# First GEMM stage in plain float32, and the conditioning row read from HBM: one change to a two-layer encoder kernel

## The chip, the cores and the metric

The kernel runs on one core of a Trainium2 chip. The metric is device time in microseconds (us) of one execution; a kernel's time is the median of its runs.

## The reference, cut to what matters

```python
cond = jax.nn.silu(c)                                   # c: (1, 2048)
for l in range(2):
    mod = (cond @ ada_w[l] + ada_b[l])[:, None, :]      # 2048 -> 6 * 2048
    sh1, sc1, g1, sh2, sc2, g2 = jnp.split(mod, 6, axis=-1)
    h = rmsnorm(x, norm_mix_g[l]) * (1 + sc1) + sh1     # x: (1, 256, 2048)
    m = hybrid_mixer(h, ...) if l == 0 else mamba2_bidirectional(h, ...)
    x = x + g1 * m
    h = rmsnorm(x, norm_ffn_g[l]) * (1 + sc2) + sh2
    x = x + g2 * squared_relu_mlp(h, ffn_w1[l], ffn_w2[l])
return rmsnorm(x, final_norm_g)
```

All inputs are float32. `hybrid_mixer` begins with `h @ w_in`; the first GEMM stage of the kernel works out the 2048 of its columns that make `v` (1024) and the two latents (512 each).

## The kernel before

Activations lie feature-major: `x` is 16 tiles of 128 features by 256 tokens. Weights come from HBM in chunks of 1024 KB ([128, 2048] float32, `load`, line 164), one DMA each on SyncE's queue, in one fixed order, into a ring of slots (`slot`, line 153): three in a permanent pool and some that a stage adds. A slot is loaded again when its last reader is done, and the queue issues in order.

Products are made with split operands. `next_half` (line 169) cuts a chunk into halves: ScalarE rounds a half to the matmul's fast float32 form (`whi`, line 177), and VectorE subtracts to get the rest (`wlo`, line 179). The activation is split the same way into the two planes of an `A` tile (`split_into`, line 281). A product is then three fast matmuls: high by high, high by low, low by high. `look` lets halves be made some way ahead of their products.

The modulation `cond @ ada_w` is done mostly on VectorE: for each of 192 tiles of the transposed `ada_w` (1024 KB each), `ada_sum` (line 323) multiplies by the row `cond`, which stands on all 128 partitions, and sums along the row in one instruction (line 325). `spread_cond` (line 126) makes that row twice, at the start and in layer 1 (line 1120): for each of 16 groups of 128 features, VectorE scales the identity by a column of silu(c) (line 132), TensorE multiplies it by a constant matrix (line 133), and ScalarE copies four results at a time from PSUM (line 134).

The stage that the change is about is `start` (line 533). Its contraction has 16 steps `kt`, a step being one chunk of `w_st`: columns 0 to 1023 for v, 1024 to 2047 for the latents. In each step `feed` keeps the normed tiles two ahead: for tile t, `by_tile` (line 450) has the two modulation tiles (scale, then shift) loaded and summed, adds the biases in three tiny VectorE instructions, and `h_tile` (line 413) makes the normed, scaled, shifted tile (VectorE line 415, ScalarE line 422) and its split (lines 282, 283). Then TensorE does v with the activation stationary and 512 weight columns moving (12 matmuls, line 569), and the latents with the weights stationary and 256 tokens moving (24 matmuls, line 204). So a step takes three loads of 1024 KB. In steps 14 and 15 the first three tiles of the next modulation rows are queued too. The raw ring has 8 slots here (3 permanent, 3 from the layer's pool, 2 from the stage's pool `sp`).

The order of instructions on each engine is set by a scheduler that lists them by its own estimates, within the program's dependences; each engine then runs its list in order.

Of the kernel before, what the change touches and what calls it, by code (L numbers as in the profile page):

```python
# [25 lines left out]
# columns of the packed per-feature parameters  # L26
# [11 lines left out]
# columns of the packed constants  # L38
# [4 lines left out]
# the modulation row that the tensor engine works out  # L43
ON_PE = (0, G1)
# the rows whose bias comes with the tile's use
# [4 lines left out]
def tile_trunk(  # L50
# [3 lines left out]
    cT_d: bass.AP,  # L54
    pos: bass.AP,
# [30 lines left out]
    def pair():  # L86
        """a slot of the second activation pool, for plain float32"""
        return acts["B"].tile([P, 2, S], F32, name="B")
# [5 lines left out]
    # ---------------------------------------------------------------- setup  # L94
# [11 lines left out]
    nc.sync.dma_start(prm, prm_d)  # L106

# [13 lines left out]
    # silu(c), a feature a partition, and as a row on every partition  # L121
# [4 lines left out]
    def spread_cond(pool):  # L126
        cond = pool.tile([P, D], F32, name="cond")
        for i in range(4):
            pc = bank()
            for j in range(4):  # L130
                dg = ev.tile([P, P], F32, name="dg", bufs=2)
                nc.vector.tensor_scalar(dg, ident, condT[:, 4 * i + j:4 * i + j + 1], float(D), op0=ALU.mult, op1=ALU.mult)
                nc.tensor.matmul(pc[:, j * P:(j + 1) * P], avg[D], dg, start=True, stop=True)  # L133
            nc.scalar.copy(cond[:, i * 512:(i + 1) * 512], pc)
        return cond

    # ------------------------------------------------------------- weights
    # Chunks come in one fixed order; their split halves are made some halves ahead of the products.
    stream = {"src": [], "next": 0, "cur": [], "halves": [], "used": 0, "look": 2}
    for a in (w_st, w_hyb, *((w_f1[0, :32], w_f2[0, :32], w_f1[0, 32:], w_f2[0, 32:])), w_ssm, w_so,  # L140
              *((w_f1[1, :32], w_f2[1, :32], w_f1[1, 32:], w_f2[1, 32:]))):
        stream["src"] += [a[i] for i in range(a.shape[0])]

    # slots of each kind: so many in the pool, and some that a stage adds
    rings = {"raw": [0], "whi": [0], "wlo": [0]}

    def more(*pools):
        """pools with more slots, and how many of each kind"""
# [35 lines left out]
    def chunk():  # L184
        """the next chunk, as the index of its first half"""
# [3 lines left out]
    def cut(w, a, n):  # L189
        """columns a .. a + n of a chunk, (high, low)"""  # L190
# [8 lines left out]
    def mm(o, w, s, act, first, last, clear=True):  # L199
        """clear: the first product resets its bank, so only the first of two tiles in a bank may"""  # L200
# [28 lines left out]
    def gemm4(hl, n=None, spare=True, feed=None, hook=None, single=False):  # L229
        """four output tiles at once, the contraction outermost"""  # L230
# [15 lines left out]
    def gemm16(hl, feed):  # L246
        """sixteen output tiles at once, two to a bank, the contraction outermost"""
# [41 lines left out]
    # ------------------------------------------------------- adaLN modulation  # L289
# [3 lines left out]
    def ada_unit(l, j, t):  # L293
        m = mod[l, j]
        raw = load(ada[(l * 6 + j) * KT + t])
        if (l, j) == ON_PE and t < KT // 2:
            # two tiles of the contraction, two rows of 512 columns each, one to a group of the array's columns
# [25 lines left out]
    def ada_sum(l, j, t, raw):  # L323
        m = mod[l, j]
        ins = nc.vector.scalar_tensor_tensor(  # L325
            raw, raw, 1.0, state["cond"], op0=ALU.mult, op1=ALU.mult, accum_out=m[:, t:t + 1]
        )
        if state["pin"]:
            # not before what a stage's start waits for
# [6 lines left out]
    def ada_queue(js, over, skip=0):  # L336
        """spread over some chunks, after the first ones"""
# [10 lines left out]
    def ada_held():  # L348
        """the sums of the units that were only loaded"""
# [16 lines left out]
    # ----------------------------------------------------------------- norms  # L366
# [8 lines left out]
    def tables():  # L375
        """the set with both functions of rsqrts, loaded here"""
        tc.keep_in_program_order(nc.scalar.preload_act_table_set("natural_log_exp_and_others"))

    def rsqrts(rs, vs, eps):
        """1/sqrt(v + eps): from the tables, then one Newton step"""  # L380
# [10 lines left out]
    def colmean(parts, n):  # L391
        """mean over the partitions and the parts [P, S], on all partitions"""
# [767 lines left out]
def _layout(inp):  # L1160
# [5 lines left out]
    def cols(v):  # L1166
        return np.asarray(v).reshape(-1, P).T
# [119 lines left out]
```

## Time and profile before

| | us |
|---|---|
| median of 3 runs | 2604.89 |
| the runs | 2596.29, 2604.89, 2606.36 |
| span of the profiled execution | 2594.1 |

The profiled execution has no time listed apart from its span; the span, from the first to the last instruction, is 2.2 us under the fastest run. TensorE is busy for 2503.8 us of it (97%), VectorE for 2053.3 (79%), ScalarE for 1371.9 (53%), and the DMA engines moved 256 GB/s on average.

How to read the profile: "L325" is line 325 of the kernel before. A group of instructions is named by line, engine, operation and `output<-inputs`. A row of the timeline gives start, length, engine, line, operation, count, and in brackets the engine's idle time before it and what ended it. A row of windows gives, for a stretch of time, each engine's busy time, the TensorE clock that was granted (1.00 is 2.4 GHz, 0.50 is 1.2 GHz), the busy share of the 16 DMA engines and what they moved in GB/s. A row of waits gives an engine and line, what it waited for, the total, the count and the longest wait. In the profile a plain float32 matmul stands as two MATMUL records, a fast one as one.

### The profile page before, as it was taken

Reading aid. Unit: us, or ns where it says so; the run is one execution under the profiler, and the core shown is the slowest. Engines: PE = TensorE matmul, PEld = TensorE weight load, DVE = VectorE, ACT = ScalarE, POOL = GpSimd, SP = SyncE. Lnnn points to the kernel's source line nnn. Section 1 sums busy time; section 2 is a strip of 40 time slices with the busy share of each in tenths; the row PEclk is TensorE's granted clock in tenths of the full one; section 3 lists DMA queues with packets and bytes.
Section 4 is the critical chain, followed back from the end, with each engine's and each line's share of the span. In section 5 each row is a group of like instructions: output and inputs, shape, how many; then the busy total and the mean of one; then the engine's idle time right before and its main releaser. Section 6 shows DMA issues by size and latency. Waiting matters only on the chain.

```text
span 2594.1 us, 41365 instructions
## 1 busy us (share of the span) xinstructions
PE 2503.8 (97%) x16616; PEld 2275.4 (88%) x16616; DVE 2053.3 (79%) x3117; ACT 1371.9 (53%) x2147; POOL 44.6 (2%) x81
## 2 busy tenths in 40 slices
PE   5779999999999999999999999999999999999998
PEld 4669899988888888889999999888898888888887
DVE  8889878898879988879898989878748865566554
ACT  4336455554334544458787878744535433444443
POOL 0000000000000000001000000000000000000000
PEclk8889999999999999999999999999999999999999
DMA  9988776779888888856656666479556775555553
GB/s 365 341 308 308 304 295 259 311 296 341 321 337 322 329 332 324 334 204 200 206 196 195 195 196 196 146 261 346 220 181 259 292 275 195 188 186 194 191 184 112
DMA packets 94801, 664.55 MB, mean 256 GB/s; under 512 B 10704, under 2 KB 10960, under 8 KB 16656
## 3 DMA queue, kind: packets, MB, share of 16 engines
q1 hardware_dynamic: 89424, 643.29, 66.6%
q0 software_dynamic: 5184, 18.61, 3.1%
q8 instruction: 130, 2.13, 0.3%
q14 instruction: 63, 0.52, 0.1%
HBM read 659.63 MB, written 2.23 MB: 255 GB/s over the span
## 4 chain that ended last, share of the span: by engine, by line
PE 90%; DVE 6%; ACT 2%; issue 1%; DMA 0%; DVEq 0%; SPq 0%; ACTq 0%
PE o L209 35%; PE o L204 27%; PE o L210 18%; PE m L204 3%; DVE raw L325 2%; PE p L1043 1%; DVE wlo L179 1%; PE p L204 1%; PE o L720 1%; ACT whi L177 1%; PE m L569 0%; PE o L770 0%; DVE B L283 0%; DVE s L481 0%; PE m L133 0%
## 5 line engine op out<-in xcount | busy, mean ns | idle before, releaser
L177 ACT CAST whi<-raw 128x1024 fp32r<-128x1024 f32 x834 | 873.7, 1051 | 944.4 <-PE o L209 575.8
L179 DVE TENSOR_TENSOR wlo<-raw,whi 128x1024 fp32r<-128x1024 f32 x834 | 1015.9, 1222 | 412.2 <-ACT whi L177 409.7
L209 PE MATMUL o<-B,whi 128*128 128x512 f32 x2194 | 762.3, 392 | 0.0
L204 PE MATMUL o<-A,whi 128*128 128x256 f32 x3648 | 675.8, 287 | 1.4 <-ACT whi L177 1.4
L209 PE MATMUL o<-A,whi 128*128 128x512 f32 x1760 | 613.1, 393 | 0.0
L210 PE MATMUL o<-B,wlo 128*128 128x256 f32 x2194 | 611.5, 279 | 0.0
L204 PEld LDWEIGHTS o<-A,whi 128*128 128x128 f32 x3648 | 576.0, 194 | 11.2 <-issue 6.6
L204 PE MATMUL o<-A,wlo 128*128 128x256 f32 x1824 | 518.4, 284 | 0.8 <-DVE wlo L179 0.8
L209 PEld LDWEIGHTS o<-B,whi 128*128 128x128 f32 x2194 | 410.8, 187 | 92.7
L210 PE MATMUL o<-A,wlo 128*128 128x256 f32 x1760 | 490.4, 279 | 0.5 <-DVE wlo L179 0.5
L325 DVE SCALAR_TENSOR_TENSOR raw<-raw,cond 128x2048 f32<-128x2048 f32 x184 | 420.1, 2284 | 4.5 <-DMA raw<-in_ada_dram 4.2
L210 PEld LDWEIGHTS o<-B,wlo 128*128 128x128 f32 x2194 | 413.4, 188 | 0.0
L209 PEld LDWEIGHTS o<-A,whi 128*128 128x128 f32 x1760 | 329.7, 187 | 74.6 <-issue 0.8
L204 PEld LDWEIGHTS o<-A,wlo 128*128 128x128 f32 x1824 | 351.8, 193 | 2.2 <-issue 1.0
L210 PEld LDWEIGHTS o<-A,wlo 128*128 128x128 f32 x1760 | 331.4, 188 | 1.8 <-DVE wlo L179 1.3
L465 DVE SCALAR_TENSOR_TENSOR x<-o,mod,x 128x256 f32<-128x256 f32 x171 | 82.0, 482 | 54.6 <-PE o L210 39.0
L204 PE MATMUL o<-B,whi 128*128 128x256 f32 x670 | 122.8, 285 | 0.3 <-ACT B L282 0.3
L204 PEld LDWEIGHTS o<-B,whi 128*128 128x128 f32 x670 | 104.6, 192 | 3.7 <-issue 2.6
L1025 DVE SCALAR_TENSOR_TENSOR ww<-ww,dtT,cb 128x256 f32<-128x256 f32 (+1 forms) x256 | 95.1, 411 | 8.0 <-ACT ww L1022 7.8
L204 PE MATMUL o<-B,wlo 128*128 128x256 f32 x335 | 94.8, 284 | 0.0
L864 DVE SCALAR_TENSOR_TENSOR s<-xp,hcw,s 128x256 f32<-128x256 f32 x192 | 92.2, 480 | 1.2
L569 PE MATMUL m<-whi,A 128*128 128x512 f32 x96 | 43.5, 513 | 48.6 <-ACT A L282 33.2
(286 smaller groups left out, 2026.1 us busy)
## 6 DMA issues: line engine op xcount, KB each, us to landing
raw<-in_w_f_dram SPq DMA_DIRECT2D x256, 1024.0 KB, 4.8
raw<-in_ada_dram SPq DMA_DIRECT2D x192, 1024.0 KB, 6.1
raw<-in_w_ssm_dram SPq DMA_DIRECT2D x81, 1024.0 KB, 4.9
raw<-in_w_hyb_dram SPq DMA_DIRECT2D x32, 1024.0 KB, 6.4
raw<-in_w_so_dram SPq DMA_DIRECT2D x32, 1024.0 KB, 4.9
raw<-in_w_st_dram SPq DMA_DIRECT2D x16, 1024.0 KB, 6.8
cu<-cumD POOLq DMA_DIRECT2D x32, 512.0 KB, 5.5
x<-in_xT_dram SPq DMA_DIRECT2D x4, 512.0 KB, 8.0
```

Of the source, the lines that this page charges most:

```text
L177: nc.scalar.copy(hi, r)
L179: nc.vector.tensor_tensor(lo, r, hi.bitcast(F32), op=ALU.subtract)
L204: nc.tensor.matmul(o, a, act[:, b, :], start=clear and first and n == 0, stop=last and n == 2, skip_group_check=True,)
L209: nc.tensor.matmul(o, hi, flat(act), start=first, stop=False, skip_group_check=True)
L210: nc.tensor.matmul(o[:, :S], lo, act[:, 0, :], start=False, stop=last, skip_group_check=True)
L325: ins = nc.vector.scalar_tensor_tensor(raw, raw, 1.0, state["cond"], op0=ALU.mult, op1=ALU.mult, accum_out=m[:, t:t + 1])
L465: nc.vector.scalar_tensor_tensor(x[:, t, :], o[:, i * S:(i + 1) * S], g[:, t:t + 1], x[:, t, :], op0=ALU.mult, op1=ALU.add)
L569: nc.tensor.matmul(ov[tt][ch], hl[kt][:, a, s], b, start=kt == 0 and n == 0, stop=kt == KT - 1 and n == 2, skip_group_check=True,)
L720: nc.tensor.matmul(o, a, lat[kt][:, b, :], start=kt == 0 and n == 0, stop=kt == 3 and n == 2, skip_group_check=True,)
L864: nc.vector.scalar_tensor_tensor(v, xp[:, i:i + S], hcw[:, ch * 5 + i:ch * 5 + i + 1], v, op0=ALU.mult, op1=ALU.add)
L1025: nc.vector.scalar_tensor_tensor(w[:, tt, c0:c1], w[:, tt, c0:c1], dtT[:, tt, d * 64 + h:d * 64 + h + 1], self.cb[:, tt, c0:c1], op0=ALU.m ...
L1043: nc.tensor.matmul(py[hh * 64:(hh + 1) * 64, i0:i1], self.xT[:, tt, c0:c0 + 64], self.ws[t, hh][:, tt, w0:w0 + i1 - i0], start=n == 0, sto ...
```

## The change

Five things change.

- In `start` the weights of the stage are no longer split. A step loads its chunk with `load(w_st[kt])` and multiplies it as it is, in plain float32, with a float32 tile `h32` (4 slots): 4 matmuls of 512 columns for v, 8 of 256 for the latents. The tile is still split into an `A` tile, for the products after the stage. The stage's pool gives 4 slots of the raw ring instead of 2 raw, 1 `whi` and 1 `wlo`, so the ring has 10.
- `w_st` leaves the stream of split chunks; the first three halves of the next chunks are made in the last step.
- `spread_cond` loads the row c from HBM onto 128 partitions with a DMA on GpSimd's queue, and makes 2 silu(c) there: tanh on ScalarE into PSUM, one VectorE instruction for each 512 columns. The factor 1/2 goes into `ada_sum`.
- The 1 of `1 + scale` is added to the bias columns once (three instructions of 128x16), and `by_tile` uses two tiny instructions instead of three.
- A new input `cr` holds c as a row.

```diff
+    for l, j in BY_TILE:
+        if j in (SC1, SC2):
+            v = prm[:, PC["adab"][0] + (l * 6 + j) * KT:PC["adab"][0] + (l * 6 + j + 1) * KT]
+            nc.vector.tensor_scalar(v, v, 1.0, None, op0=ALU.add)
...
     def spread_cond(pool):
         cond = pool.tile([P, D], F32, name="cond")
+        nc.gpsimd.dma_start(cond, cr_d[0].partition_broadcast(P))
         for i in range(4):
+            v = cond[:, i * 512:(i + 1) * 512]
             pc = bank()
-            for j in range(4):
-                dg = ev.tile([P, P], F32, name="dg", bufs=2)
-                nc.vector.tensor_scalar(dg, ident, condT[:, 4 * i + j:4 * i + j + 1], float(D), op0=ALU.mult, op1=ALU.mult)
-                nc.tensor.matmul(pc[:, j * P:(j + 1) * P], avg[D], dg, start=True, stop=True)
-            nc.scalar.copy(cond[:, i * 512:(i + 1) * 512], pc)
+            nc.scalar.activation(pc, v, AF.Tanh, scale=0.5)
+            nc.vector.scalar_tensor_tensor(v, pc, 1.0, v, op0=ALU.add, op1=ALU.mult)
         return cond
...
-    for a in (w_st, w_hyb, *((w_f1[0, :32], w_f2[0, :32], w_f1[0, 32:], w_f2[0, 32:])), w_ssm, w_so,
+    for a in (w_hyb, *((w_f1[0, :32], w_f2[0, :32], w_f1[0, 32:], w_f2[0, 32:])), w_ssm, w_so,
...
         ins = nc.vector.scalar_tensor_tensor(
-            raw, raw, 1.0, state["cond"], op0=ALU.mult, op1=ALU.mult, accum_out=m[:, t:t + 1]
+            raw, raw, 0.5, state["cond"], op0=ALU.mult, op1=ALU.mult, accum_out=m[:, t:t + 1]
         )
...
-        nc.vector.tensor_scalar(gs, gs, bias(l, jc, t), 1.0, op0=ALU.add, op1=ALU.add)
-        nc.vector.tensor_tensor(gs, gs, pr(name, t), op=ALU.mult)
+        nc.vector.scalar_tensor_tensor(gs, gs, bias(l, jc, t), pr(name, t), op0=ALU.add, op1=ALU.mult)
         nc.vector.tensor_tensor(sh, sh, bias(l, jh, t), op=ALU.add)
...
-            more((pool, dict(raw=3)), (sp, dict(raw=2, whi=1, wlo=1)))
+            more((pool, dict(raw=3)), (sp, dict(raw=4)))
...
-            hl = []
+            hl, h32 = [], []
             def feed(k):
                 while len(hl) < min(k + 2, KT):
-                    hl.append(h_tile(len(hl), r, *by_tile(0, "mix0", SC1, SH1, len(hl))))
+                    t = len(hl)
+                    gs, sh = by_tile(0, "mix0", SC1, SH1, t)
+                    n = sp.tile([P, S], F32, name="h32", bufs=4)
+                    nc.vector.tensor_tensor(n, x[:, t, :], r, op=ALU.mult)
+                    nc.scalar.activation(n, n, AF.Identity, bias=sh, scale=gs)
+                    h32.append(n)
+                    hl.append(split(n, "A"))
...
-                w = chunk()
+                w = load(w_st[kt])
                 for ch in range(2):
-                    hi, lo = cut(w, ch * 512, 512)
                     for tt in range(2):
-                        s = slice(tt * P, (tt + 1) * P)
-                        for n, (a, b) in enumerate(((0, hi), (0, lo), (1, hi))):
-                            nc.tensor.matmul(
-                                ov[tt][ch], hl[kt][:, a, s], b,
-                                start=kt == 0 and n == 0, stop=kt == KT - 1 and n == 2, skip_group_check=True,
-                            )
+                        nc.tensor.matmul(
+                            ov[tt][ch], h32[kt][:, tt * P:(tt + 1) * P], w[:, ch * 512:(ch + 1) * 512],
+                            start=kt == 0, stop=kt == KT - 1, skip_group_check=True,
+                        )
                 if kt == KT - 1:
                     more((pool, dict(raw=3)))
+                    for _ in range(3):
+                        next_half()
                 for m in range(8):
-                    mm(oq[m], w, 8 + m, hl[kt], kt == 0, kt == KT - 1, m % 2 == 0)
+                    nc.tensor.matmul(
+                        oq[m], w[:, (8 + m) * P:(9 + m) * P], h32[kt],
+                        start=kt == 0 and m % 2 == 0, stop=kt == KT - 1, skip_group_check=True,
+                    )
```

What this does to the order of instructions is shown at three places (a row: line, operation, `output<-inputs` with buffer numbers, shape).

VectorE in the middle of `start`, one step, before (`raw` is a modulation or weight chunk, `mod01` and `mod00` the scale and shift, `A` the split tile):

```order
L179 TENSOR_TENSOR wlo_474<-raw_470,whi_472 128x1024
L283 TENSOR_TENSOR A_450<-s_448,A_450 128x256
L179 TENSOR_TENSOR wlo_534<-raw_470,whi_532 128x1024
L325 SCALAR_TENSOR_TENSOR raw_500,mod01_101<-raw_500,cond_117 128x2048
L415 TENSOR_TENSOR s_1014<-x_82,rstd_205 128x256
L455 TENSOR_SCALAR mod01_101<-mod01_101,prm_87 128x1
L325 SCALAR_TENSOR_TENSOR raw_503,mod00_100<-raw_503,cond_117 128x2048
L456 TENSOR_TENSOR mod01_101<-mod01_101,prm_87 128x1
L457 TENSOR_TENSOR mod00_100<-mod00_100,prm_87 128x1
```

and with the change:

```order
L331 SCALAR_TENSOR_TENSOR raw_440,mod01_104<-raw_440,cond_120 128x2048
L461 SCALAR_TENSOR_TENSOR mod01_104<-mod01_104,prm_87 128x1
L331 SCALAR_TENSOR_TENSOR raw_443,mod00_103<-raw_443,cond_120 128x2048
L557 TENSOR_TENSOR h32_504<-x_82,rstd_165 128x256
L462 TENSOR_TENSOR mod00_103<-mod00_103,prm_87 128x1
L289 TENSOR_TENSOR A_451<-h32_448,A_451 128x256
```

The two subtractions of the weights' low halves are gone, and the subtraction that splits the tile (now line 289) serves a tile two steps older.

SyncE's queue at the end of `start`, before; the last chunk of `w_st` is the first row but one:

```order
L166 DMA raw_1069<-in_ada_dram 128x2048
L166 DMA raw_1097<-in_w_st_dram 128x2048
L166 DMA raw_1127<-in_ada_dram 128x2048
L166 DMA raw_1130<-in_ada_dram 128x2048
L166 DMA raw_1142<-in_ada_dram 128x2048
L166 DMA raw_1145<-in_ada_dram 128x2048
L166 DMA raw_1148<-in_ada_dram 128x2048
L166 DMA raw_1167<-in_w_hyb_dram 128x2048
```

and with the change:

```order
L172 DMA raw_594<-in_w_st_dram 128x2048
L172 DMA raw_608<-in_ada_dram 128x2048
L172 DMA raw_611<-in_ada_dram 128x2048
L172 DMA raw_622<-in_ada_dram 128x2048
L172 DMA raw_625<-in_ada_dram 128x2048
L172 DMA raw_628<-in_ada_dram 128x2048
L172 DMA raw_631<-in_w_st_dram 128x2048
L172 DMA raw_645<-in_w_st_dram 128x2048
L172 DMA raw_651<-in_w_hyb_dram 128x2048
```

The last two chunks of `w_st` now stand behind the last five modulation tiles; `raw_645` is the 51st load of 1024 KB in the queue.

ScalarE where layer 1 makes the row `cond` again, before:

```order
L282 CAST B_17932<-B_16149 128x256
L282 CAST B_17943<-B_16149 128x256
L134 COPY cond_18247<-m_18248 128x512
L134 COPY cond_18247<-m_18262 128x512
L372 ACTIVATE s_17808<-B_17782 128x256
```

and with the change:

```order
L183 CAST whi_17336<-raw_17308 128x1024
L139 ACT_TABLE_LOAD
L139 ACTIVATE m_17665<-cond_17663 128x512
L183 CAST whi_17364<-raw_17362 128x1024
L139 ACTIVATE m_17668<-cond_17663 128x512
```

The copies that waited for TensorE are tanh activations that wait for a DMA, with a table load ahead of them, between the casts that feed TensorE.

## Rows read from the trace of the kernel before

**Rows 1.** The page: busy time of TensorE and VectorE, share of the span, instructions.
```profile
PE 2503.8 (97%) x16616; PEld 2275.4 (88%) x16616; DVE 2053.3 (79%) x3117; ACT 1371.9 (53%) x2147; POOL 44.6 (2%) x81
```

**Rows 2.** Windows: length, busy us (count) of five engines, PEclk, DMA share, GB/s.
```profile
0.00:10.00 10.00, 1.97 (x6) 1.43 (x6) 1.76 (x10) 2.86 (x5) 1.43 (x6) 1.00 0.70 199
10.00:40.00 30.00, 13.86 (x44) 10.28 (x45) 27.20 (x58) 14.67 (x23) 0.00 (x0) 0.72 1.02 422
40.00:50.00 10.00, 8.50 (x60) 7.81 (x58) 9.38 (x18) 4.08 (x6) 0.00 (x0) 0.99 1.00 389
40.00:180.00 140.00, 106.79 (x564) 91.61 (x562) 120.31 (x169) 43.55 (x63) 0.00 (x0) 0.87 0.88 332
200.00:260.00 60.00, 60.00 (x480) 55.57 (x478) 56.07 (x93) 37.34 (x59) 0.00 (x0) 1.00 0.86 332
```

**Rows 3.** The chain of waits inside the stage: start us, us, what.
```profile
100.31 2.22 DVE raw L325 x2
102.96 2.22 DVE raw L325 x2
105.40 0.61 ACT s L422
...
108.56 1.22 DVE wlo L179
```

**Rows 4.** VectorE groups in one step, 100.22 to 109.69 us: count | busy us, mean ns | idle.
```profile
L325 DVE SCALAR_TENSOR_TENSOR raw<-raw,cond 128x2048 f32<-128x2048 f32 x2 | 4.6, 2284 | 0.0
L179 DVE TENSOR_TENSOR wlo<-raw,whi 128x1024 fp32r<-128x1024 f32 x3 | 3.6, 1220 | 0.5 <-ACT whi L177 0.5
```

**Rows 5.** Timeline of TensorE: plain float32 matmuls of 256 columns.
```profile
204.12 0.60 PE L664 MATMUL m<-accq,avg 128*128 128x256 f32 x2
204.55 0.59 PE L665 MATMUL m<-acck,avg 128*128 128x256 f32 x2
```

**Rows 6.** Timeline of TensorE: the first matmul, and after two later waits.
```profile
34.12 1.65 PE L569 MATMUL m<-whi,A 128*128 128x512 f32 x3 [15.35 <-ACT whi L177]
...
51.36 0.80 PE L569 MATMUL m<-whi,A 128*128 128x512 f32 x1 [2.86 <-ACT A L282]
...
56.68 0.63 PE L204 MATMUL o<-A,whi 128*128 128x256 f32 x2
...
106.48 0.50 PE L569 MATMUL m<-whi,A 128*128 128x512 f32 x1 [1.99 <-ACT A L282]
109.33 0.40 PE L204 MATMUL o<-A,whi 128*128 128x256 f32 x2
...
112.08 0.28 PE L204 MATMUL o<-A,wlo 128*128 128x256 f32 x1
```

**Rows 7.** Timeline of ScalarE: the scaled and shifted tile 0.
```profile
26.51 0.60 ACT L422 ACTIVATE s<-s,mod,mod 128x256 f32<-128x256 f32 x1 [4.03 <-DVE s L415]
```

**Rows 8.** The page: DMA issues, KB each, median us to landing.
```profile
cu<-cumD POOLq DMA_DIRECT2D x32, 512.0 KB, 5.5
```

**Rows 9.** Timeline of TensorE: the end of the stage and the products after it.
```profile
179.96 0.28 PE L204 MATMUL o<-A,wlo 128*128 128x256 f32 x1
181.69 0.50 PE L204 MATMUL o<-A,whi 128*128 128x256 f32 x2 [1.45 <-ACT whi L177]
```

**Rows 10.** Waits, 1665 to 1690 us: total, times, longest.
```profile
PE m L133 <- DVE dg L132: 1.3, 3, 1.0
PE p L1043 <- ACT cond L134: 0.7, 1, 0.7
```

**Rows 11.** Timelines of TensorE and ScalarE in layer 1, around the second row.
```profile
1722.77 0.61 PE L133 MATMUL m<-dg,avg 128*128 128x128 f32 x4
1723.14 0.48 PE L209 MATMUL o<-A,whi 128*128 128x512 f32 x1
...
1667.56 1.28 ACT L377 ACT_TABLE_LOAD   x1
1711.57 1.05 ACT L177 CAST whi<-raw 128x1024 fp32r<-128x1024 f32 x1 [1.77 <-PE o L209]
```

More of the change, by code (lines that the diff above doesn't have):

```diff
@@ L54, in tile_trunk @@
     cT_d: bass.AP,
+    cr_d: bass.AP,
     pos: bass.AP,
@@ L1154, in tile_trunk @@
         nc.sync.dma_start(out[:, i:j, :], v)
-_ORDER = ["xT", "cT", "pos", "prm", "cst", "wsT", "bs", "ada", "w_st", "w_hyb", "w_f1", "w_f2", "w_ssm", "w_so"]
+_ORDER = ["xT", "cT", "cr", "pos", "prm", "cst", "wsT", "bs", "ada", "w_st", "w_hyb", "w_f1", "w_f2", "w_ssm", "w_so"]
 def _layout(inp):
@@ L1198, in _layout @@
     a["cT"] = cols(inp["c"])
+    a["cr"] = inp["c"]
     a["pos"] = inp["positions"]
```

## The prediction

> **What bounds the kernel now.** I read the page first, then the busy time of each engine in stretches, then the chain of waits, then single instructions. On the page TensorE is busy for 97% of the span [rows 1], so in most of the kernel only TensorE's own time counts. The stretches show where this is not so. From 200 us on TensorE is busy for 60.00 of 60 us at the full clock; from 40 to 180 us, in the stage that is changed, for only 106.79 of 140, at a mean granted clock of 0.87, while VectorE is busy for 120.31 [rows 2]. The chain of waits says what holds the stage: modulation sum, modulation sum, the scaled tile on ScalarE, the cast of the weights, the subtraction of their low half, and again from the top [rows 3]. One step of the contraction takes 9.47 us (the same instruction stands at 100.22 and 109.69 us, the bounds of [rows 4]); two sums take 4.6 us of it and each low half 1.22 [rows 4]. So VectorE and its round trip to ScalarE pace the stage, and its last product ends at 179.96 + 0.28 = 180.2 us [rows 9]. After that TensorE waits 1.45 us for a cast [rows 9] and then is the bound until the end. What the stage gains or loses comes through to the end, unless the next stage takes it back.
>
> **The change part by part.**
>
> VectorE. A step loses two low halves (2 x 1.22 us) and a tiny instruction, and with the cast gone the wait for it. What is left is two sums, 4.6 us, two instructions of 256 columns, and small ones: 9.47 - 2.44 leaves at most 7.0 us, less the waits of the old round trip. The new tile feeds the products straight from ScalarE, the split for later products is two tiles late in the list, so nobody waits for it. VectorE stops being the bound.
>
> DMA comes next. Up to the last chunk of the stage 51 loads of 1.0486 MB are queued (32 modulation tiles, 3 of the next rows, 16 chunks), 53.5 MB. With x (2.1), parameters, constants and positions (0.6) and the new row on 128 partitions (1.05) that makes 57.2 MB. By 10 us 1.99 MB have moved (199 GB/s); where loads queue up, 422 GB/s move for 30 us and 389 for the next 10 [rows 2], a mean of 414. I take this, because ten slots now keep loads queued: the load that wants a chunk's slot is ten loads later, 25 us, while TensorE has used the chunk 7 us after it landed, or 17 when it lags by a step and a half. The remaining 55.2 MB take 133.3 us, so the last chunk lands at 143.3 us and the one before it, 2.53 us earlier, at 140.8. A step is three loads, 7.6 us.
>
> TensorE. Two plain float32 matmuls of 256 columns start 0.43 us apart [rows 5]. The trace has none with 512 columns on the whole array; bounds are 0.43 us, if the width did not count, and 1.72 us, twice the double at half clock. I take the double, 0.86, since the fast matmuls go by width: 12 of 512 columns in 2.85 us, 0.24 each, and the 24 of 256 that follow in (112.08 + 0.12 - 109.33), 0.12 each [rows 6]. A step is then 8 x 0.43 + 4 x 0.86 = 6.88 us at the full clock, more than before but under 7.6. The first product needs only the scaled tile 0, which ScalarE starts at 26.51 us [rows 7], and not a cast: it starts near 28 us instead of 34.12 [rows 6]. From a wait the engine comes back at half clock: after 2.86 us idle the 12 matmuls of v took 5.32 us (51.36 to 56.68), after 1.99 us idle 2.85 us (106.48 to 109.33) [rows 6]. So a fall of the clock costs 2.5 us. TensorE alone would end at 28 + 16 x 6.88 + 2.5 = 140.6 us, before the DMA allows it.
>
> The end of the stage is therefore set by the last two chunks. They now stand behind the last five modulation tiles in the queue; six loads separate chunks 13 and 14, 15.2 us, in which TensorE works 6.88 and idles. It starts step 14 at 140.8 us at half clock and ends both at 140.8 + 2 x 6.88 + 2.5 = 157.1 us. Against 180.2 that is **23.1 us** less. At 422 GB/s and without the fall of the clock it would be 138.3 + 13.8 = 152.1, a gain of 28; at 389 GB/s throughout 149.2 + 16.3 = 165.5, a gain of 15.
>
> The Trainium skill (DMA: Bandwidth & Descriptors, section "Where 436 GB/s comes from") says that for transfers from HBM to SBUF a core's share of HBM, about 358 GB/s, is what binds. The 422 GB/s over 30 us speak against it here, with one core running. By that rule the stage would end near 178 us and the gain would be 3 us; this is a mechanism among the rivals.
>
> The row at the start. Sixteen small VectorE instructions, 16 matmuls and four copies go; a DMA of 1 MB, four tanh and four VectorE instructions of 512 columns come. The squares of x wait behind the tanh on ScalarE, and x shares the DMA engines with the row, 1.05 MB or 2.5 us. I cost this at nothing beyond the bytes counted, because the stage waits for DMA; if that cover went, it is some 3 us at TensorE's first product.
>
> The row in layer 1. Two of the 16 matmuls hold TensorE for 0.37 us (1722.77 to 1723.14) [rows 11], so all hold it for 3.0; it waits 1.3 us for the diagonal tiles and 0.7 us for the copies [rows 10]. Gone, that is up to 5 us. What comes is on ScalarE: a table load of 1.28 us [rows 11] and a wait for the DMA, whose nearest row is 5.5 us for 512 KB [rows 8]. The casts behind it run ahead of TensorE and wait 1.77 us for it in each turn [rows 11], with three halves made ahead, so TensorE should not feel a single delay of that size. I take 3 us of gain, between 5 and a loss of 2.
>
> Tiny instructions and bias columns: nothing, since VectorE waits for loads now.
>
> **Sum.** 23.1 + 3 = 26 us. The profiled span of 2594.1 would be 2568. The profile stands near the fastest run (2596.29); the median is 10.8 us over the span, so the median goes from 2604.89 to **2579 us**.
>
> **The rivals.**
>
> The DMA engines do not keep the rate for 130 us. For it: over the whole stage they were busy for 0.88 and moved 332 GB/s [rows 2], which is 377 at full share. Against it: 422 with a full queue. At 377 the last chunks land at 153.6 and 156.4, the stage ends at 170, the gain is 10 + 3: 2592 us. At 332 it would end at 189 and the kernel would take 2611.
>
> TensorE stays at half clock, the rival on the slower side. At 1.2 GHz a step takes 13.76 us; the stage would end at 28 + 16 x 13.76 = 248 us, 68 later: 2670 us with layer 1's gain. It decides from a step of (180.2 - 28) / 16 = 9.5 us, 1.38 times my 6.88. For it: the clock was below full for parts of this stage, mean 0.87 [rows 2], and the price of 512 columns is not shown. Against it: a slow TensorE has no waits left, and after 5.3 us of unbroken work the clock had risen [rows 6].
>
> In between, the clock falls at every step, since TensorE now waits for DMA at each: 6.88 + 2.5 = 9.4 us a step, an end at 178 us, 2600 us. Against it: the wait of a step is 7.6 - 6.88 = 0.7 us, and after 1.99 us the clock had held [rows 6]. The Trainium skill (TensorE: Matmul & The Clock Gate, section "HAM oscillation — how this bites in real kernels") describes this pattern, a wait for data ahead of each tile of the contraction and a slow start of each; the row with 1.99 us does not agree for waits so short.
>
> The next stage takes gain back: VectorE is busy there for 56.07 of 60 us [rows 2], its sums are the same, but the third chunk after the stage needs the slot of the stage's last chunk. Half the gain would be left, 2592 us.
>
> That the change does not do what it says is excluded by the order of instructions.
>
> **How the numbers follow.** My forecast has 0.70, its own range being 2572 to 2590 (the ends above, with 5 and 0 us for layer 1). DMA at a lower rate has 0.14, half clock throughout 0.07, a fall at every step 0.04, the next stage 0.05. A measurement of this kernel can tell about 0.5%, 13 us, from no change. Below 2592 lie the forecast and a third of the lower rates: 0.75. Over 2618 lies half clock: 0.07, with 0.01 for DMA at the old mean and layer 1 going wrong. The rest, 0.17, is within 0.5%. The range runs from 2562, since runs spread by 10 us and a median may fall near the fastest, to 2600, which takes in the rivals within 0.5%.
>
> **What would show it.** Right: steps of about 7.6 us in the stage's middle, a DMA share near 1.0 from 10 to 140 us, plain matmuls of 512 columns 0.86 us apart, TensorE's wait ahead of step 14, an end of the stage near 157 us, no diagonal products at the start or in layer 1. Wrong: steps of 9 us or more with a full clock (a rate or a price misread), a granted clock of 0.50 through the stage, VectorE without idle time in it, or the products after the stage starting late on their weights.

## The result and the profile after

The changed kernel takes 2580.39 us, the median of 6 runs (2568.93 to 2590.82), against 2604.86 (2592.11 to 2606.64) of the kernel before, run beside it: a ratio of 0.990 with an interval of 0.987 to 0.993. The forecast was 2579, and "faster" by over 0.5% was its likeliest case. The profiled execution took 2579.52 us, with a span of 2577.8.

The page has TensorE as busy as before ([rows 1]), with 256 matmul records fewer.

```profile
PE 2503.8 (97%) x16360; PEld 2242.0 (87%) x16360; DVE 2010.5 (78%) x3016; ACT 1345.8 (52%) x2118; POOL 45.6 (2%) x83
```

The windows of the changed kernel (columns as in [rows 2]) show the stage with another bound. From 10 to 140 us the DMA engines are full, at 420 to 421 GB/s; TensorE has a clock of 1.00 in the middle, where it had 0.87 over the stage, and VectorE is busy for 38.27 of 50 us.

```profile
0.00:10.00 10.00, 0.00 (x0) 0.00 (x0) 0.67 (x6) 1.50 (x2) 1.42 (x6) 1.00 0.75 234
10.00:40.00 30.00, 13.34 (x35) 7.72 (x36) 27.81 (x53) 13.94 (x23) 0.00 (x0) 1.00 1.01 420
50.00:100.00 50.00, 47.33 (x159) 29.35 (x158) 38.27 (x57) 7.03 (x14) 0.00 (x0) 1.00 1.01 421
100.00:140.00 40.00, 32.07 (x113) 20.72 (x111) 32.35 (x45) 5.02 (x10) 0.00 (x0) 0.97 1.01 421
200.00:260.00 60.00, 60.00 (x459) 56.12 (x458) 55.69 (x106) 28.71 (x44) 0.00 (x0) 1.00 0.72 267
```

TensorE's timeline answers to [rows 6] and [rows 9]. L577 is now v (two records make a matmul of 512 columns), L586 the latents, L210 the products after the stage.

```profile
28.74 4.44 PE L577 MATMUL m<-raw,h 128*128 128x512 f32 x6 [7.25 <-ACT h L558]
...
37.33 2.74 PE L577 MATMUL m<-raw,h 128*128 128x512 f32 x6
39.90 1.02 PE L577 MATMUL p<-raw,h 128*128 128x512 f32 x2
40.76 3.62 PE L586 MATMUL o<-h,raw 128*128 128x256 f32 x16
44.21 2.74 PE L577 MATMUL m<-raw,h 128*128 128x512 f32 x6
...
80.82 2.81 PE L577 MATMUL m<-raw,h 128*128 128x512 f32 x6 [0.36 <-DMA raw<-in_w_st_dram]
88.28 2.81 PE L577 MATMUL m<-raw,h 128*128 128x512 f32 x6 [0.34 <-DMA raw<-in_w_st_dram]
...
141.22 4.50 PE L577 MATMUL m<-raw,h 128*128 128x512 f32 x6 [7.81 <-DMA raw<-in_w_st_dram]
...
149.88 2.74 PE L577 MATMUL m<-raw,h 128*128 128x512 f32 x6
...
153.31 3.62 PE L586 MATMUL o<-h,raw 128*128 128x256 f32 x16
157.69 0.50 PE L210 MATMUL o<-A,whi 128*128 128x256 f32 x2 [0.77 <-DVE B L627]
```

Three matmuls of 512 columns take 2.57 us (37.33 to 39.90), 0.857 each; a step on TensorE takes 6.88 (37.33 to 44.21); a step on DMA takes 7.46 (80.82 to 88.28), with a wait of 0.34; ahead of step 14 TensorE waits 7.81 us and comes back slowly, so that step takes 8.66 (141.22 to 149.88). The stage ends at 156.9 us, 23.3 us earlier than the 180.2 before.

To follow this to the end, I compared the starts of the same products of TensorE in both traces, counted from the last one. The changed kernel is ahead by 26.2 us at 200 us of the span of before, since TensorE had waited longer and at a lower clock behind the old stage, by 24.2 at 400, by 24.9 at 1600, by 26.8 after layer 1's second row and by 27.8 at 1900. Then it falls back, evenly, to 16.6 at 2550. (These differences are good to some 0.2 us.) This last part is the second feed-forward layer, which the change does not touch. The same products run there in all of one execution at one pace and in all of another at another, with the clock at 1.00. Windows of before and of after:

```profile
2100.00:2400.00 300.00, 300.00 (x1733) 264.54 (x1732) 183.29 (x233) 131.26 (x169) 0.00 (x0) 1.00 0.56 200
```

```profile
2100.00:2400.00 300.00, 300.00 (x1699) 260.14 (x1699) 175.55 (x225) 130.53 (x172) 0.00 (x0) 1.00 0.53 187
```

In 300 us stand 1733 matmuls before and 1699 after: 346 and 353 ns for a pair (one of 512 columns, one of 256). The groups of instructions there (1900 to 2400 us) show it in the mean of the 512-column matmul, 391 ns before and 399 after:

```profile
L209 PE MATMUL o<-A,whi 128*128 128x512 f32 x760 | 263.7, 391 | 0.0
```

```profile
L215 PE MATMUL o<-A,whi 128*128 128x512 f32 x768 | 271.4, 399 | 0.0
```

Whether that is the change's doing had to be settled with the rest.

### The profile page after: what moved, and what is told of

The parts are those of the page before. It is cut to its first block, busy times and chain, and to the rows that moved or that the text cites. A ratio compares the mean times of both kernels' runs of the same rounds, so it can differ in the third digit from the quotient of the medians.

```text
span 2577.8 us, 40713 instructions
## 1 busy us (share of the span) xinstructions
PE 2503.8 (97%) x16360; PEld 2242.0 (87%) x16360; DVE 2010.5 (78%) x3016; ACT 1345.8 (52%) x2118; POOL 45.6 (2%) x83
## 4 chain that ended last, share of the span: by engine, by line
PE 90%; DVE 4%; DMA 4%; ACT 2%; issue 1%; SPq 0%; DVEq 0%; ACTq 0%
PE o L215 35%; PE o L210 27%; PE o L216 18%; PE m L210 3%; DMA raw<-in_ada_dram 2%; PE p L1056 1%; PE p L210 1%; DVE raw L331 1%; PE o L733 1%; DMA raw<-in_w_st_dram 1%; DVE wlo L185 1%; DMA prm<-in_prm_dram 0%; PE o L783 0%; DVE B L289 0%; DVE s L486 0%
## 5 line engine op out<-in xcount | busy, mean ns | idle before, releaser
L183 ACT CAST whi<-raw 128x1024 fp32r<-128x1024 f32 x802 | 840.0, 1050 | 954.3 <-PE o L215 575.6
L185 DVE TENSOR_TENSOR wlo<-raw,whi 128x1024 fp32r<-128x1024 f32 x802 | 978.4, 1223 | 420.9 <-ACT whi L183 419.1
L210 PE MATMUL o<-A,whi 128*128 128x256 f32 x3392 | 624.6, 285 | 0.8 <-DVE B L627 0.8
L210 PEld LDWEIGHTS o<-A,whi 128*128 128x128 f32 x3392 | 529.4, 192 | 9.4 <-issue 5.7
L216 PE MATMUL o<-A,wlo 128*128 128x256 f32 x1760 | 491.4, 280 | 0.5 <-DVE wlo L185 0.5
L210 PE MATMUL o<-A,wlo 128*128 128x256 f32 x1696 | 480.5, 283 | 0.0
L215 PEld LDWEIGHTS o<-A,whi 128*128 128x128 f32 x1760 | 330.8, 188 | 81.0 <-ACT whi L183 1.2
L216 PEld LDWEIGHTS o<-A,wlo 128*128 128x128 f32 x1760 | 332.1, 189 | 1.8 <-DVE wlo L185 1.4
L210 PEld LDWEIGHTS o<-A,wlo 128*128 128x128 f32 x1696 | 324.7, 192 | 0.4 <-issue 0.2
L470 DVE SCALAR_TENSOR_TENSOR x<-o,mod,x 128x256 f32<-128x256 f32 x171 | 82.1, 483 | 57.6 <-PE o L216 41.1
L210 PE MATMUL o<-B,whi 128*128 128x256 f32 x670 | 124.1, 286 | 2.7 <-DVE x L470 2.7
L210 PEld LDWEIGHTS o<-B,whi 128*128 128x128 f32 x670 | 105.4, 193 | 5.6 <-DVE x L470 2.9
L210 PE MATMUL o<-B,wlo 128*128 128x256 f32 x335 | 95.8, 286 | 0.0
L288 ACT CAST B<-s 128x256 fp32r<-128x256 f32 x128 | 50.1, 406 | 43.9 <-DVE s L486 43.3
```

What stands on the lines that cost most here:

```text
L183: nc.scalar.copy(hi, r)
L185: nc.vector.tensor_tensor(lo, r, hi.bitcast(F32), op=ALU.subtract)
L210: nc.tensor.matmul(o, a, act[:, b, :], start=clear and first and n == 0, stop=last and n == 2, skip_group_check=True,)
L215: nc.tensor.matmul(o, hi, flat(act), start=first, stop=False, skip_group_check=True)
L216: nc.tensor.matmul(o[:, :S], lo, act[:, 0, :], start=False, stop=last, skip_group_check=True)
L288: nc.scalar.copy(hl[:, 0, :], a)
```

## The experiments

Theory: the stage's gain is the plain float32 form's; DMA bounds the stage then, and its end hangs on the place of the last two chunks in the queue; the row gains little. Rivals: VectorE or TensorE still sets the step; the row at the start does part of it; the next stage takes gains back; and, for the last 11 us, that the change slows the feed-forward layer. "Ahead" below is always against the changed kernel, by the same products, unless said otherwise.

**The row alone, on the kernel before.**

```diff
         cond = pool.tile([P, D], F32, name="cond")
+        nc.gpsimd.dma_start(cond, cr_d[0].partition_broadcast(P))
         for i in range(4):
...
-            raw, raw, 1.0, state["cond"], op0=ALU.mult, op1=ALU.mult, accum_out=m[:, t:t + 1]
+            raw, raw, 0.5, state["cond"], op0=ALU.mult, op1=ALU.mult, accum_out=m[:, t:t + 1]
```

> Edit: the kernel before with the row from HBM alone; the first stage keeps its split weights. Theory (the stage's gain is the plain float32 form's, the row is worth 2 us and that in layer 1): the first product starts within 3 us of the 34.12 us before, a step stays at 9.47 us, the stage's last product ends at 180 us plus or minus 2, and from layer 1's second row on the kernel runs 2 us ahead of the kernel before; some 2600 us. Rival (the row does part of the stage's work, because the diagonal instructions at the start held VectorE and TensorE): the stage ends 3 us or more earlier than 180 us.

It took 2593.83 us. TensorE's timeline:

```profile
152.01 0.50 PE L569 MATMUL m<-whi,A 128*128 128x512 f32 x1 [1.99 <-ACT A L282]
161.47 0.51 PE L569 MATMUL m<-whi,A 128*128 128x512 f32 x1 [2.02 <-ACT A L282]
...
179.56 0.50 PE L204 MATMUL o<-A,whi 128*128 128x256 f32 x2 [1.33 <-ACT whi L177]
```

A step is still 9.46 us and the stage ends at 178.2, 2 us earlier than before: the theory holds, and the 23 us are not the row's. They belong to the rest of the change, the plain form above all; the tiny instructions were not tried alone. By 350 us those 2 us were gone and 1.9 more; over the products at the second row in layer 1 it went from 1.1 behind to 1.5 ahead of the kernel before, so the row there was worth 2.6 us in this pair. The time is lower than the 2600 expected because both feed-forward layers ran at the faster pace (below); at that pace the kernel before takes 2592.1 to 2596.3 us, so the row alone shows no gain in time.

**Diagonal rows in the changed kernel.**

```diff
-        nc.gpsimd.dma_start(cond, cr_d[0].partition_broadcast(P))
         for i in range(4):
-            v = cond[:, i * 512:(i + 1) * 512]
             pc = bank()
-            nc.scalar.activation(pc, v, AF.Tanh, scale=0.5)
-            nc.vector.scalar_tensor_tensor(v, pc, 1.0, v, op0=ALU.add, op1=ALU.mult)
+            for j in range(4):
+                dg = ev.tile([P, P], F32, name="dg", bufs=2)
+                nc.vector.tensor_scalar(dg, ident, condT[:, 4 * i + j:4 * i + j + 1], 2.0 * D, op0=ALU.mult, op1=ALU.mult)
+                nc.tensor.matmul(pc[:, j * P:(j + 1) * P], avg[D], dg, start=True, stop=True)
+            nc.scalar.copy(cond[:, i * 512:(i + 1) * 512], pc)
```

> Edit: the changed kernel with the row made by diagonal tiles again, in both places. Theory (DMA bounds the stage, so the row's 1.05 MB at the start cost 2.5 us there): the last chunk lands 2.5 us earlier and the stage ends near 154.4 us in place of 156.9; in layer 1 the 2 us that the row gained are gone again; in all 0 to 1 us from the changed kernel. Rival (the diagonal tiles cost more at the start than the bytes they save, since squares and sums queue behind them): the stage ends at 156.9 us or later, 2 us or more slower in all.

It took 2579.64 us. TensorE's timeline:

```profile
138.08 4.72 PE L578 MATMUL m<-raw,h 128*128 128x512 f32 x6 [7.79 <-DMA raw<-in_w_st_dram]
...
154.77 0.51 PE L211 MATMUL o<-A,whi 128*128 128x256 f32 x2 [0.77 <-DVE B L628]
```

Without the row's 1.05 MB the chunk of step 14 lands 3.1 us earlier and the stage ends at 154.0, 2.9 us earlier: at the start the row from HBM costs about what its bytes cost (2.5 us at 421 GB/s). The rest of the account was not as expected. Of the 2.9 us the mixer left 0.6 at 400 us, and the diagonal row in layer 1 cost 0.7 us (from 11.06 to 11.75 behind, the first layer's pace included), not 2.

**The three loads behind the last chunks.**

```diff
-                if kt == KT - 2:
-                    state["todo"] = first
-                    for _ in range(3):
-                        ada_unit(*state["todo"].pop(0))
...
                     for _ in range(3):
                         next_half()
+                    state["todo"] = first
+                    for _ in range(3):
+                        ada_unit(*state["todo"].pop(0))
```

> Edit: the changed kernel with the first three tiles of the next modulation rows queued behind the last chunks of the stage, not between them. Theory (the end of the stage is set by the last two chunks' place in the queue): three loads fewer ahead of them, 7.5 us; TensorE waits no 7.8 us ahead of step 14, its clock does not fall there, and the stage ends at 147 to 148 us, 9 us earlier than 156.9. Half of it or more may be lost behind the stage, if the three tiles or the next stage's chunks come late. Rival (the stage's DMA is not in the order of the queue, or the next stage waits for the moved tiles as long): the stage ends as early or the products behind it start later, and the kernel takes 2580 us as the changed one does.

It took 2568.08 us. TensorE's timeline:

```profile
134.10 2.81 PE L573 MATMUL m<-raw,h 128*128 128x512 f32 x6 [0.15 <-DMA raw<-in_w_st_dram]
...
144.49 3.62 PE L585 MATMUL o<-h,raw 128*128 128x256 f32 x16
151.06 0.50 PE L210 MATMUL o<-A,whi 128*128 128x256 f32 x2 [2.95 <-DVE B L626]
```

The wait of 7.81 us is gone, step 14 runs at full speed and the stage ends at 148.1 us, 8.8 earlier: the queue's order set its end. But at 400 us only 0.2 us is left (that the time is 11 us lower is the pace of the last layer, below). A part of the loss is seen at once. In the changed kernel VectorE's sums of these tiles run while it waits for DMA anyway:

```profile
133.65 2.29 DVE L331 SCALAR_TENSOR_TENSOR raw<-raw,cond 128x2048 f32<-128x2048 f32 x1
...
138.74 2.28 DVE L331 SCALAR_TENSOR_TENSOR raw<-raw,cond 128x2048 f32<-128x2048 f32 x1
...
147.16 3.71 DVE L185 TENSOR_TENSOR wlo<-raw,whi 128x1024 fp32r<-128x1024 f32 x3 [5.87 <-ACT whi L183]
155.15 0.48 DVE L627 SCALAR_TENSOR_TENSOR B<-o,prm,B 128x256 fp32r<-128x256 f32 x1 [4.28 <-ACT B L626]
```

In the experiment they stand between the splits of the latents, for which TensorE waits:

```profile
144.56 2.29 DVE L331 SCALAR_TENSOR_TENSOR raw<-raw,cond 128x2048 f32<-128x2048 f32 x1 [0.18 <-DMA raw<-in_ada_dram]
...
148.31 2.28 DVE L331 SCALAR_TENSOR_TENSOR raw<-raw,cond 128x2048 f32<-128x2048 f32 x1
...
150.53 0.48 DVE L626 SCALAR_TENSOR_TENSOR B<-o,prm,B 128x256 fp32r<-128x256 f32 x1
```

**Half of each load.**

```diff
-                w = load(w_st[kt])
+                w = slot("raw", D)
+                nc.sync.dma_start(w[:, :HALF], w_st[kt][:, :HALF])
...
-                        oq[m], w[:, (8 + m) * P:(9 + m) * P], h32[kt],
+                        oq[m], w[:, m * P:(m + 1) * P], h32[kt],
```

> Edit: the changed kernel with only the first 1024 columns of each chunk of the stage loaded; the latents use the weights of v, so the latents' own weights are left out of the computation. TensorE's and VectorE's work is the same, DMA has 2.5 chunks for a step in place of 3, 6.2 us. Theory (DMA bounds a step, TensorE's 6.88 us is next): the stage has no regular waits for its chunk, TensorE runs at 6.88 us a step and the last chunks land 20 us earlier; the stage ends at 28.7 + 16 x 6.88 = 139 to 143 us, 14 to 18 us earlier than 156.9. Rival (VectorE's two sums and what stands between them, or TensorE, set the step): the stage ends within 3 us of 156.9.

It took 2567.92 us. TensorE's timeline:

```profile
132.51 2.74 PE L578 MATMUL m<-raw,h 128*128 128x512 f32 x6
135.09 1.02 PE L578 MATMUL p<-raw,h 128*128 128x512 f32 x2
135.94 3.62 PE L587 MATMUL o<-h,raw 128*128 128x256 f32 x16
141.51 0.51 PE L210 MATMUL o<-A,whi 128*128 128x256 f32 x2 [1.95 <-DVE B L628]
```

With the same instructions and fewer bytes TensorE has no wait for a chunk; the stage ends at 139.6, 17.4 us earlier. So DMA was the bound, and neither VectorE nor TensorE. Of this, 11.6 us are left at 400 us and at the end.

**Eight slots instead of ten.**

```diff
-            more((pool, dict(raw=3)), (sp, dict(raw=4)))
+            more((pool, dict(raw=3)), (sp, dict(raw=2)))
```

> Edit: the changed kernel with 8 slots of the raw ring in the first stage in place of 10. Theory (the ring of ten keeps loads queued; 25 us lie between a load and the reuse of its slot): with eight, 20 us, the queue still does not run dry, 421 GB/s from 10 to 140 us and the stage ends at 156 to 158 us. Rival (two slots fewer leave gaps: a chunk that TensorE holds blocks the queue, which issues in order): the DMA share falls under 0.97 in the stage and it ends 3 us or more later than 156.9.

It took 2581.08 us: 421 GB/s from 10 to 140 us, an end at 157.2. In the stage the ring was not at its limit.

**The three loads between the last two chunks.**

```diff
-                if kt == KT - 2:
+                if kt == KT - 1:
                     state["todo"] = first
                     for _ in range(3):
                         ada_unit(*state["todo"].pop(0))
```

> Edit: the changed kernel with the first three tiles of the next modulation rows queued between the last two chunks of the stage, in place of ahead of both. The run with all three behind both ended the stage 8.7 us earlier, but kept 1 us of it: the three sums, 6.9 us of VectorE, stood between the norming of the latents. Theory (that is why it was given back): here the sums run where VectorE waits for DMA, at 134 to 142 us; the chunk of step 14 lands at 133, that of step 15 at 143; TensorE waits 3 us ahead of step 15, the stage ends at 150.5 to 152 us, 5 to 6 us earlier than 156.9, and 4 us or more of it is still there at 400 us. Rival (any time gained in the stage is given back in the mixer, which VectorE bounds until 320 us): the offset to the changed kernel at 400 us is under 1.5 us.

It took 2578.94 us. TensorE's timeline:

```profile
144.22 4.48 PE L577 MATMUL m<-raw,h 128*128 128x512 f32 x6 [2.80 <-DMA raw<-in_w_st_dram]
...
149.39 3.62 PE L586 MATMUL o<-h,raw 128*128 128x256 f32 x16
153.78 0.39 PE L210 MATMUL o<-A,whi 128*128 128x256 f32 x1 [0.77 <-DVE B L627]
```

The stage ends at 153.0, 3.9 us earlier (step 15 lost time to the clock), and no sum stands between the latents. Yet 0.4 us is left at 400 us (and 0.2, not the 1 us of the expectation, in the run with all three behind). My theory of the loss fell here: the three sums are not the reason, or not all of it.

**The same, with the diagonal row at the start alone.**

```diff
-        state["cond"] = spread_cond(c1)
+        state["cond"] = spread_diag(c1)
```

(`spread_diag` is the row by diagonal tiles, as above.)

> Edit: as the run before it, and the row at the start by diagonal tiles again (layer 1 keeps the row from HBM). Theory: 2.5 to 3 us less DMA, so the stage ends at 148 us, 9 us earlier than the changed kernel, and 6 us or more of it is there at 400 us. Rival (the mixer gives it back): under 1.5 us at 400 us, as the other run would also show.

It took 2584.16 us. TensorE's timeline:

```profile
141.00 2.81 PE L588 MATMUL m<-raw,h 128*128 128x512 f32 x6 [2.82 <-DMA raw<-in_w_st_dram]
...
150.10 0.50 PE L221 MATMUL o<-A,whi 128*128 128x256 f32 x2 [1.97 <-DVE B L638]
```

The stage ends at 148.1, and 5.3 us are left at 400 us: less than the theory's 6, far more than the rival's 1.5. A second profile of the same kernel, below, has 3.4 there.

**One load between the chunks, two behind.**

```diff
                 if kt == KT - 1:
                     state["todo"] = first
-                    for _ in range(3):
-                        ada_unit(*state["todo"].pop(0))
+                    ada_unit(*state["todo"].pop(0))
...
                         next_half()
+                    for _ in range(2):
+                        ada_unit(*state["todo"].pop(0))
```

> Edit: the changed kernel with one of the three tiles between the last two chunks and two behind them. Theory (VectorE's sums between the latents give the gain back): TensorE has no wait in the last steps, the stage ends at 147.5 us, 9.4 us earlier, but two sums, 4.6 us, stand where the latents are normed, so that 3 us at most are kept at 400 us. Rival (DMA's order alone counts): as much is kept as in the run with all three between the chunks, or more.

It took 2578.58 us. The stage ends at 147.5, 9.4 us earlier; 1.6 us are left. That is under 3, but also more than with all three between the chunks, and the two differ by less than two profiles of one kernel do (below). So it does not tell the theories apart.

Part of what is taken back has a place, if not yet a cause: the end of the mixer, 300 to 330 us (in the kernel before the same products stand 28 us later, at 330 to 360). Windows there of before, after, the run with the loads between the chunks, and the run with half of each load:

```profile
330.00:360.00 30.00, 29.42 (x221) 27.60 (x220) 24.94 (x43) 18.14 (x36) 0.53 (x1) 1.00 0.75 280
```

```profile
300.00:330.00 30.00, 27.03 (x192) 24.86 (x185) 22.20 (x37) 17.26 (x34) 0.53 (x1) 0.94 0.83 313
```

```profile
300.00:330.00 30.00, 24.48 (x171) 22.84 (x171) 20.28 (x38) 16.34 (x33) 0.53 (x1) 0.94 0.74 272
```

```profile
300.00:330.00 30.00, 27.14 (x209) 26.66 (x210) 21.85 (x33) 14.21 (x21) 0.00 (x0) 0.94 0.71 262
```

TensorE has 0.6 us of idle time there before and 3 us after, with its clock under 1.00 too (0.94). The waits, in the same window begun at 260 us, are for the residual's first tile, and in the experiment for the attention's copies as well; of after:

```profile
PE o L210 <- DVE x L470: 2.7, 1, 2.7
```

and of the run with the loads between the chunks:

```profile
PE o L210 <- DVE x L470: 2.7, 1, 2.7
PE m L825 <- ACT t L822: 1.7, 2, 1.0
```

| against the changed kernel, us | stage's end | at 400 us |
|---|---|---|
| diagonal rows | -2.9 | -0.6 |
| loads behind the last chunks | -8.8 | -0.2 |
| half of each load | -17.4 | -11.6 |
| eight slots | +0.3 | +2.0 |
| loads between the chunks | -3.9 | -0.4 |
| the same, diagonal start | -8.8 | -5.3 |
| the same kernel, second profile | -7.0 | -3.4 |
| one between, two behind | -9.4 | -1.6 |
| the changed kernel, second profile | +0.3 | +0.4 |

From 260 to 340 us the runs of the table that gained on the stage lose 1.3 to 4.0 us, but the run with half of each load only 0.2. It is not the only place: that run had lost 5.6 us, and the run with the loads behind the last chunks 5.1, by 260 us. Why each part takes so much was not tried: it would take kernels that hold the order of that part fixed.

**The best of these, and the changed kernel again, timed.**

> The kernel with the row by diagonal tiles at the start and the three loads between the last two chunks, timed. In its first profile it was 5.3 us ahead of the changed kernel at 400 us, and both feed-forward layers ran at 353.3 ns for a pair of matmuls (each pair 512 and 256 columns) where the changed kernel's first ran at 346.8. Theory (each feed-forward layer of each execution, of any of these kernels, runs at one of these two paces, 10.5 us apart, and the edits have no part in it): times near 2563, 2573.5 and 2584 us and none between, by 0, 1 or 2 slow layers, 4 to 5 us under the changed kernel's times of 2569, 2579.5 and 2590. Rival (the queue's order makes the feed-forward slow): all times at 2584.

> The changed kernel itself, timed again on the same chip beside the one before it. Theory: times at 2569, 2579.5 and 2590 us within 1.5 us, by 0, 1 or 2 slow feed-forward layers, and its profile shows the number that its time says (the mean of a 512-column matmul near 399 ns in a slow layer, 391 to 394 in a fast one). Rival (the spread is something else, a clock or DMA rate): times between these levels, or a profile whose number of slow layers does not fit its time.

Both ran unedited: the first is the run with the diagonal start and the loads between the chunks. It took 2576.35 us (median of 6; ratio to before 0.9907, interval 0.9871 to 0.9942), the changed kernel 2573.79 (0.9888, 0.9854 to 0.9922). The intervals overlap: no version is shown to beat the changed kernel. In the second profile of the best version the clock fell in step 15, behind a wait about as long as the one behind which it had held in the first:

```profile
141.12 4.51 PE L588 MATMUL m<-raw,h 128*128 128x512 f32 x6 [2.84 <-DMA raw<-in_w_st_dram]
```

So two profiles of one kernel differ by 1.8 us at the stage's end and by 1.9 at 400 us, and differences of under 2 us at 400 us in the table above say nothing of an edit. The single times, sorted by level, with all runs of the kernel before:

| layers at 353 ns | none | one | both |
|---|---|---|---|
| before (19 runs) | 2592.1 to 2596.3 (6) | 2604.4 to 2606.6 (11) | 2617.8, 2618.0 |
| changed (12) | 2567.8 to 2568.9 (4) | 2579.0 to 2581.5 (6) | 2589.7, 2590.8 |
| best (6, and its first run) | 2564.6 | 2574.8 to 2576.6 (3) | 2584.2 to 2589.2 (3) |

The column is read from the time; for the profiled runs it can be read from the trace too. Each of 12 profiles (before, after and ten experiments) has each of its two feed-forward layers at a mean distance of 346.8 or 353.3 ns from pair to pair, and none between; 10 of the 24 layers are at 353.3. Their numbers fit the times: in the run of the changed kernel that took 2579.0 us it was the first layer, in that of 2579.52 the second. Groups in the first layer (700 to 1100 us) and the second (1900 to 2400) of the repeated run:

```profile
L215 PE MATMUL o<-A,whi 128*128 128x512 f32 x512 | 181.0, 399 | 0.0
...
L215 PE MATMUL o<-A,whi 128*128 128x512 f32 x768 | 266.5, 394 | 0.0
```

So the pace changes with the execution and not with the edit; the rival, that the queue's order makes the layer slow, falls with 2564.6. Level by level the best version lies 3.5 to 4.3 us under the changed kernel (means), as its lead at 400 us says (5.3 us in its first profile, 3.4 in its second); only one of its runs stands at the first level. The theory's levels were 1.6 to 2.8 us too low, and they are broader than it said: 2587.0 and 2589.2 lie 3.0 and 5.2 us over 2584, and 2581.5 of the changed kernel lies 2.0 us from 2579.5, where 1.5 was allowed.

## Why the prediction was right

**At equal pace the change is worth 25.5 to 27.6 us; the sum said 26.** From the table, level by level: means of 2594.4 and 2568.3, 2605.6 and 2580.1, 2617.9 and 2590.3. The medians first compared both lie at one such layer, hence 24.5. The prediction put the 10.8 us between the profile of before and its median down to a spread; it was one layer's pace.

**The sum was in part luck.** In the traces the lead grows as 23.3 us at the stage's end (forecast 23.1), 2.9 more right behind it, 2.0 lost again by 400 us, 0.7 won by 1600, 2.0 at layer 1's row (forecast 3) and 1.0 by 1900. What the next stage gives and takes was put at nothing in the sum, and the two pieces, 2.9 and 2.0, nearly cancel.

**VectorE stops being the bound; DMA is.** Right, by the windows and by the run with half of each load. The DMA share is 1.01 from 10 to 140 us, as forecast.

**DMA's time.** Two errors cancelled. The rate was 421 GB/s, not 414, which would bring the chunk of step 14 some 2.2 us earlier than 140.8; but at 141.22 us, when TensorE could start, 2.3 + 131.2 x 0.421 = 57.6 MB had moved, 1.4 MB more than stood ahead of it in the queue and of itself (56.2 MB). By these bytes later loads had moved alongside the chunk, and it landed that much later. The step was 7.46 us for 7.6.

**TensorE.** The price between 0.43 and 1.72 us was taken as 0.86 and is 0.857; a step 6.88 as forecast; the start 28.74 for 28; the wait ahead of step 14 7.81 for 15.2 - 6.88 = 8.3; the clock's price 1.78 us (8.66 - 6.88) for 2.5. That price was read from one of the dearest steps: in the trace of before the 12 matmuls of v took 4.0 to 5.3 us in the slow steps, 1.1 to 2.5 more than the 2.85 of the others, and the runs with a slow step 14 or 15 paid 1.7 to 2.9. The end, 156.9 for 157.1.

**The row at the start.** Costed by its bytes, right: the chunk of step 14 lands 3.1 us earlier in the run without it, against 2.5 forecast from the rate.

**The row in layer 1.** Mis-sized: 3 us forecast, 2.0 in the pair of traces (24.86 to 26.84 ahead), 2.6 and 0.7 in the two other pairs. The matmuls and the waits for diagonal tiles went, but the mixer's weights, `ww`, come later. Waits between 1640 and 1800 us of the changed kernel:

```profile
PE p L1056 <- DVE ww L1042: 2.4, 1, 2.4
PE o L215 <- ACT whi L183: 1.0, 1, 1.0
```

In [rows 10] 2.0 us of waits stand there. I named what would go, and not what is late next.

**The rivals.** DMA at a lower rate, refuted by 421 GB/s over 130 us. By the rule of the Trainium skill (DMA: Bandwidth & Descriptors, section "Where 436 GB/s comes from"), a core's share of about 358 GB/s binds; this trace does not agree, with one core running. Half clock throughout, refuted by 1.00. (The argument against it read too much from [rows 6]: the row at 56.68 us, 0.63 us for two matmuls where the row at 109.33 has 0.40, is still slow.) A fall at every step: behind waits of 0.3 us the 512-column matmuls kept their 2.8 us for six records. The Trainium skill (TensorE: Matmul & The Clock Gate, section "HAM oscillation — how this bites in real kernels") describes such a fall behind each wait for data, in a kernel whose waits are longer than the 0.3 us of a step here. In the runs with the change the slow start came at the first product (4.44 us for six records, behind 7.25), behind 7.8 us, and behind 2.80 and 2.84, while a step behind 2.82 ran at full speed. I had argued with the wait of 1.99 us behind which the clock held; in the same trace it fell behind one of 2.00, and the 12 matmuls took 4.35 us:

```profile
97.02 0.50 PE L569 MATMUL m<-whi,A 128*128 128x512 f32 x1 [2.00 <-ACT A L282]
...
101.37 0.50 PE L204 MATMUL o<-A,whi 128*128 128x256 f32 x2
```

So the argument did not hold, though the rival was wrong: the waits were 0.3 us, and behind these the clock held. The next stage taking gain back: it took some, 2 us between 200 and 400 us, not half, because the shorter waits and the full clock behind the stage had brought 3 us on top. For every further gain in the stage it was the right rival: of 3 to 9 us it left 0.2 to 5.3.

## What to carry to other kernels

When a stage's work is dropped, price the next bound by its own rows: bytes in the queue by a rate at which it was seen full, and the place of the last load that the stage needs. A gain at a stage's end is not yet a gain: follow the same instruction through both traces to a place where TensorE never waits before crediting it. And where times come in levels, find what the levels are before comparing medians of a few runs; here two layers, worth 10 to 12 us each, hide an edit worth 4.

## What had not been expected

A feed-forward layer of some 600 us of unbroken matmuls, alternately of 512 and 256 columns, runs at 346.8 or 353.3 ns a pair, through all of the layer, with a granted clock of 1.00 and no wait in either. Both values occur in both layers, in the same kernel run twice and under the edits. In a slow layer two of three pairs take some 350 ns and the third some 360; in a fast one they take 342 to 351, but for the few where the sequence changes. What sets it stays open.
